# Expert-choice block on one core: another order of places for the streamed expert weights, and other moments and queues for three small loads

## Chip, cores, metric

One Trainium2 chip, one core of it. The time is that of one execution on the device, in microseconds; before and after are medians over runs. The profile is of one execution.

## What is computed

A diffusion block on 512 latent and 256 context tokens of width 1024 (float32, one layer). Two head groups (RWKV-7, 8 heads of 64, in both directions; gated linear attention) mix the tokens, an output projection and a norm follow, and then an expert-choice mixture of 16 SwiGLU experts (inner width 2816), each on its best 64 tokens:

```python
x = ln_affine(DN_ALPHA * x + g1 * (o_lat @ w_out), ln1_g, ln1_b)
h2 = modulate(ln_plain(x), sh2, sc2)
aff = softmax(h2 @ router_w)                       # (512, 16)
gates, idx = top_k(aff.T, 64)                      # each expert picks 64 tokens
y_e = (silu(h2[idx] @ w_gate[e]) * (h2[idx] @ w_up[e])) @ w_down[e]     # for 16 experts
x = ln_affine(DN_ALPHA * x + g2 * scatter_add(gates * y_e), ln2_g, ln2_b)
```

The expert weights are 16 x 3 x 1024 x 2816 float32 numbers, 553.6 MB; each is read once.

## The kernel before

One function, `body`, writes the whole program; a scheduler orders the instructions of each engine by their dependences and by priorities (`H(name)` raises one), and each engine then runs its list in order. Memory comes from pools in which a later tile takes the place of an earlier one and waits for the earlier one's last reader.

The stages that matter here:

- **Recurrence, to about 746 us.** RWKV runs over four strips of two heads (`b` = 0 to 3). Per strip: elementwise work (`rw_elem`, which loads two small weight tiles, `e_wr` and `e_ws`, in pool `zp0`), keys, an inverse of 24 triangular blocks (`rw_inverse`, L863 to L949) and twelve steps (`rw_step`, L969 to L1047), each of which needs the state of the step before. With strip 3 the scheduler fills TensorE's pauses with parts of the output projection.
- **Output projection, L1163 to L1210.** Its weights for heads 0 to 3 of the mix are eight tiles `w00` to `w31` (512 KB each, first number the 128 rows, second the column half), loaded by GpSimd at L1171. `product` (L1094) multiplies them, in three products each, since both sides are split into a high and a low part. Rows of x (`kx`, L1163) and gate rows (`zgs`, L1054) are loaded by SyncE.
- **Norm and router, L1215 to L1370.** For the four token tiles, in the order 1, 2, then 0, 3: statistics (L1247, L1255), norm with the factors `l1g` and `l1b` (each 128 x 1024, read broadcast from 4 KB; GpSimd's L1271 and VectorE's L1272 for tiles 1 and 2, VectorE's L1267 and L1274 for 0 and 3), second norm (L1263, L1265), transpose (L1343), router logits with `rwt` (L1348), softmax, and ranks by counting (L1303). `rwt` is made from the raw router weights `rwr` (128 x 8 x 16) by L1233 and L1242. L1366 is filler on TensorE that reads `hT` and `lgs`.
- **Experts, L1381 on.** `route(e)` gathers an expert's 64 tokens with one-hot products; `product_` multiplies them by eight gate tiles and eight up tiles of 128 x 2816 (L1439 loads, L1446 multiplies), then eight tiles of the down matrix follow (L1489, L1494). All are loaded by SyncE, in order, one tile after another, into twelve places of 12 KB per partition, `w0` to `w11`, which are taken round by round in the order of `wslot`. The places lie over what the earlier stages used: `w4`, `w5`, `w6` over arrays that the inverse of strip 3 reads last; `w7`, `w8`, `w9` over the recurrence's own of strips 1 and 3; `w0` to `w3` over the output projection's operands; `w10` over `hT` and `lgs`; `w11` over what the ranking reads.

A load waits until its place is free, and so does every load behind it on the same queue. SyncE's queue holds, in this order before the experts: the zgs loads (the last of them waits for strip 2's gate), `l1g` and `l1b` (which wait for the last recurrence step, as their pool lies over its arrays), the router's weights, and then the expert tiles.

```python
def vec(pl, name, src):                                    # L1217
    t = pl.tile([P, D], F32, name=name)
    EN[O("vq","s")].dma_start(t, src.to_broadcast([P, D]))
wslot = itertools.cycle((7, 8, 6, 4, 5, 2, 3, 1, 0, 11, 10, 9))        # L1384
wt = wp.tile([P, F], F32, name="wt", tag=f"w{next(wslot)}")            # L1438
ld = nc.sync.dma_start(wt, v[:, k])                                    # L1439
```

Of the kernel before, what the change touches and what calls it, by code (L numbers as in the profile page):

```python
# [8 lines left out]
F32 = mybir.dt.float32  # L9
# [3 lines left out]
OP = mybir.AluOpType  # L13
PSUM = bass.MemoryType.PSUM

OPT = dict(h_load=-100,h_rho=(0, 500, 60, 400),rh=(1, 2, 2, 2),b1=(0, 4),h_step=(0, 0, 0, 200),adb=4,h_post=(100, -100, 0),gf=512,h_rows=(0, 100),h_acc0=-100,h_scores=(500, 700, 0, -50),h_keys=(400, 500, 0, -100),b3=(0, 8),sp=1,gse='v',ea=1,f7=3,h_glah=0,bz=(10, 10),f3=1,r0b=0,fb=3,ge=0,p2=2,p1=0,f5=1,h_elem=(0, 700, 0, 60),f2=3,b2=(4, 0),h_inv=(200, 0, 0, 100),wo=(5, 6, 3, 4, 1, 2, 0, 8, 7),f8=3,f1=2,f6=1,h_split=0,f4=1,h_sub=(60, 60, 0, 150),h_out=(300, -100, 0, -200),h_crit=(700, 1000, 100, 400),vu='aa',h_lev=(150, 0, 0, 0),pwr=0,h_kv=(0, 0, 0, 0),h_post3=150)


def O(n, d):
    return OPT.get(n, d)  # L20


P = 128
D = 1024
KD = 8
# [3 lines left out]
E = 16  # L29
# [7 lines left out]
def body(tc, I, out):  # L37
    nc = tc.nc
# [18 lines left out]
    EN = dict(s=nc.sync, a=nc.scalar, g=nc.gpsimd)  # L57
# [3 lines left out]
    def pool(name, side, **kw):  # L61
        c = tc.tile_pool(name=name, bufs=1, side=side, reuse_waits="tile", **kw)
        return c, c.__enter__()
# [13 lines left out]
    def pss():  # L77
        return bank("s", 3)

    def pc():  # L80
        return bank("c", 3)
# [253 lines left out]
    for i in range(2):  # L335
        a = zpp.tile([P, 10, 66], F32, name=f"zpl{i}")
# [4 lines left out]
        a = zpp.tile([P, TC + 2], F32, name=f"zpc{i}")  # L341
# [158 lines left out]
    for d in range(2):  # L500
        for i in range(2):
            la, t = t3s[0:2]
            bias = ab[:, 2 * d + i:2 * d + i + 1]
            for lo, n in ((0, TC), (TC, TL)):
                p = pss()[:, 0:n]
# [13 lines left out]
            e = ebl[:, :, d, i]  # L519
# [13 lines left out]
    c_z0, zp0 = pool("rwz0", "left")  # L533
# [10 lines left out]
    wo = I["w_out"][0].rearrange("(k p) f -> p k f", p=P)  # L544
# [18 lines left out]
    for step in range(11):  # L563
# [12 lines left out]
        p = pc()  # L576
# [156 lines left out]
    def rw_elem(b, pss, fill=lambda n: None):  # L733
        with H("elem", b):
            return rw_elem_(b, pss, fill)
# [46 lines left out]
    e = rw_elem(0, pss, fill)  # L782
# [344 lines left out]
    with after(sub[0]) if O("ea", 1) else contextlib.nullcontext():  # L1127
        e = rw_elem(1, pe)
# [4 lines left out]
    for b in range(4):  # L1133
# [6 lines left out]
        if b < 2:  # L1140
            e = rw_elem(b + 2, pe)
# [73 lines left out]
    c_o, op_ = pool("outp", "right")  # L1215
# [5 lines left out]
        return t  # L1221

    hTs = [op_.tile([P, KD, P], F32, name=f"hT{i}") for i in range(2)]
    rwt = op_.tile([P, KD, 32], F32, name="rwt")
    rwr = op_.tile([P, KD, E], F32, name="rwr")
    sel = op_.tile([P, E], F32, name="sel")
    lgs = op_.tile([P, P], F32, name="lgs")
    sts = op_.tile([P, 8, 16], F32, name="sts")
    l1g, l1b = vec(op_, "l1g", I["ln1_g"]), vec(op_, "l1b", I["ln1_b"])

    EN[O("vq","s")].dma_start(rwr, I["router_w"][0].rearrange("(k p) e -> p k e", p=P))
    G.memset(rwt, 0.0)
    V.tensor_copy(rwt[:, :, 0:E], rwr)  # L1233

# [1 line left out]
    p = pe()  # L1236
# [89 lines left out]
    for part in ((1, 2), (0, 3)):  # L1326
        v = [x.rearrange("p (a b) -> p a b", b=P)[:, part[0]:part[1] + 1:part[1] - part[0]]
             for x in (mx[3][0], mx[3][1], ym[:, 3])]
        act(v[0], v[2], AF.Copy)
        V.tensor_tensor(v[1], v[2], v[0].bitcast(F32), op=S_)  # L1330
        for t in part:
# [4 lines left out]
            sp = t in (1, 2)  # L1336
# [3 lines left out]
            for k0 in (0, 4):  # L1340
                p = pe()
# [3 lines left out]
            p = pe()  # L1345
# [33 lines left out]
    def b2(tag, bufs, n=1):  # L1379
        return ps2.tile([P, 512 * n], F32, name="ps_" + tag, tag=tag, bufs=bufs)  # L1380

    c_m, mp = pool("moe", "left")
    c_w, wp = pool("wp", "left")
    wslot = itertools.cycle((7, 8, 6, 4, 5, 2, 3, 1, 0, 11, 10, 9))  # L1384
    for i in range(12):
        wp.tile([P, 3072], F32, name=f"w{i}")
    g2b = mp.tile([P, 512], F32, name="g2b")
# [39 lines left out]
    for e in range(E):  # L1427
# [35 lines left out]
        p = b2("m", 2)  # L1463
# [12 lines left out]
        for j0, n in GR:  # L1476
            p = b2("m", 2)
# [23 lines left out]
        if e == E - 1:  # L1501
            for t in range(4):
                for c in range(2):
                    p = b2(*(("m", 2) if t == 3 else ("gu", 6)))
# [53 lines left out]
```

## Time and profile before

| | |
|---|---|
| median of 3 runs | 2110.29 us (2107.8 to 2117.51) |
| profiled execution | 2105.25 us, its span 2103.5 us |
| TensorE busy | 1831.6 us, 87% of the span |
| VectorE, ScalarE, GpSimd busy | 769.4, 481.1, 315.7 us |
| mean DMA rate over the span | 302 GB/s |
| DMA rate in the span's slices 17 to 39 (of 40) | 424 to 426 GB/s |
| products with gate and up weights (L1446) | 689.2 us busy, 47.7 idle before them |
| products with down weights (L1494) | 311.4 us busy, 31.6 idle before them |

Busy times add up the instructions of one engine; matmuls are pipelined, so a busy TensorE is not one at its peak. A slice is 52.6 us. The expert stage fills the slices from 15 on; the ones before are bound by chains of small steps.

### The profile page before, as it was taken

The page shows a single profiled execution, that of the slowest core. Times are in us where ns is not written, and L with a number is a line of the kernel's source. Part 1 is how long each engine was busy: PE and PEld are TensorE (multiplying, and loading weights), DVE is VectorE, ACT ScalarE, POOL GpSimd, SP SyncE. Part 2 cuts the span into 40 slices and gives each one's busy share as a digit, 9 for nine tenths or more (in the row PEclk, how much of TensorE's full clock was granted, in tenths as well). Part 3 has the DMA queues.
Part 4 walks back from the last instruction along what each step waited for, and adds up shares of the span by engine and source line. Part 5 has one row for each costly group of instructions (what it writes and reads, how often), then busy time and mean ns, then how long its engine had stood idle before and what let it go on. Part 6 is the DMA issues. An engine that isn't in the chain of part 4 may idle for free. (4 is left out here: it accounts for less than half of the span.)

```text
span 2103.5 us, 31329 instructions
## 1 busy us (share of the span) xinstructions
PE 1831.6 (87%) x13266; PEld 936.1 (44%) x13266; DVE 769.4 (37%) x1445; ACT 481.1 (23%) x978; POOL 315.7 (15%) x318
## 2 busy tenths in 40 slices
PE   5898997788889988999998888988988888889886
PEld 1666776666667653333333333333333332333322
DVE  4676667766663262122112112122122121121113
ACT  2242445555652441011101101010010010011001
POOL 2543656343140220000000000000000000000001
PEclk8989998888897999999999999999999999999998
DMA  7645631510000268999999999999999999999995
GB/s 276 180 147 184 216 102 45 174 46 18 2 28 7 87 269 371 424 424 425 425 425 424 425 425 425 424 425 425 425 425 424 424 425 424 425 424 424 426 424 226
DMA packets 111416, 638.50 MB, mean 304 GB/s; under 512 B 13007, under 2 KB 40248, under 8 KB 60332
## 3 DMA queue, kind: packets, MB, share of 16 engines
q1 hardware_dynamic: 108944, 625.74, 73.1%
q0 software_dynamic: 2016, 10.49, 1.5%
q8 instruction: 104, 1.70, 0.3%
q10 hardware_dynamic: 316, 0.28, 0.0%
q14 instruction: 36, 0.29, 0.0%
HBM read 619.54 MB, written 15.75 MB: 302 GB/s over the span
## 5 line engine op out<-in xcount | busy, mean ns | idle before, releaser
L1446 PE MATMUL ps_gu<-wt,xT 128*64 128x512 f32 (+1 forms) x3072 | 689.2, 568 | 47.7 <-DMA wt<-in_ex_up_dram 35.7
L1446 PEld LDWEIGHTS ps_gu<-wt,xT 128*64 128x64 f32 x3072 | 239.2, 138 | 435.3 <-issue 292.4
L1494 PE MATMUL ps_gu<-wd,hT 128*64 128x512 f32 x1408 | 311.4, 595 | 31.6 <-DMA wd<-in_ex_down_dram 31.6
L1494 PEld LDWEIGHTS ps_gu<-wd,hT 128*64 128x64 f32 x1408 | 97.3, 137 | 233.8 <-issue 173.2
L1467 ACT ACTIVATE gT<-ps_m 128x512 f32<-128x512 f32 x16 | 9.6, 597 | 602.1 <-PE ps_m L45 602.1
L1508 DVE TENSOR_TENSOR ye<-ps_gu,g2b 128x512 f32<-128x512 f32 x16 | 11.1, 692 | 372.1 <-PE ps_gu L1494 372.1
L1297 POOL MEMSET cnt<- 128x12 f32 x16 | 1.6, 107 | 884.8 <-DVE rank L1319 872.7
L1409 PE MATMUL ps_m<-h,oh 128*64 128x512 f32 x256 | 93.1, 615 | 45.9 <-DVE oh L1404 45.9
L1520 DVE TENSOR_TENSOR kx<-kx,ps_m 128x512 f32<-128x512 f32 x120 | 77.1, 684 | 152.0 <-PE ps_m L1514 152.0
L298 PE MATMUL ps_d<-hh,wh 128*128 128x512 f32 (+1 forms) x336 | 127.3, 379 | 4.2 <-ACT kx L362 3.0
L298 PE MATMUL ps_d<-hh,wl 128*128 128x512 f32 (+1 forms) x336 | 122.5, 365 | 5.3 <-POOL wl L290 5.3
L298 PE MATMUL ps_d<-hl,wh 128*128 128x512 f32 (+1 forms) x336 | 123.6, 368 | 3.4 <-POOL hl L269 3.4
L88 DVE TENSOR_SCALAR hm<-hm 128x512 f32<-128x512 f32 (+1 forms) x48 | 19.5, 405 | 180.6 <-ACT hm L1458 180.6
L1411 ACT ACTIVATE xg<-ps_m 128x512 f32<-128x512 f32 x16 | 9.6, 597 | 330.1 <-PE ps_m L1409 330.1
L290 POOL TENSOR_TENSOR wl<-raw,wh 128x1024 fp32r<-128x1024 f32 x26 | 67.4, 2592 | 93.7 <-ACT wh L289 92.8
L1418 DVE TENSOR_TENSOR xT<-ps_m,mod 128x512 f32<-128x512 f32 x16 | 11.1, 692 | 188.5 <-PE ps_m L1414 188.5
L298 PEld LDWEIGHTS ps_d<-hh,wh 128*128 128x128 f32 x336 | 66.9, 199 | 25.8 <-issue 10.1
L298 PEld LDWEIGHTS ps_d<-hh,wl 128*128 128x128 f32 x336 | 67.2, 200 | 15.1 <-POOL wl L290 5.5
L298 PEld LDWEIGHTS ps_d<-hl,wh 128*128 128x128 f32 x336 | 66.9, 199 | 14.3 <-POOL hl L269 5.1
L1514 PE MATMUL ps_m<-ye,gT 64*128 64x512 f32 x244 | 68.8, 640 | 0.0
L1409 PEld LDWEIGHTS ps_m<-h,oh 128*64 128x64 f32 x256 | 28.9, 142 | 85.4 <-issue 77.6
L1303 DVE SCALAR_TENSOR_TENSOR scr<-ps_m,aff,lo 128x128 bf16<-128x128 f32 (+3 forms) x60 | 33.1, 551 | 91.6 <-PE ps_m L1399 90.0
(454 smaller groups left out, 2669.8 us busy)
## 6 DMA issues: line engine op xcount, KB each, us to landing
wt<-in_ex_gate_dram SPq DMA_DIRECT2D x128, 1408.0 KB, 26.4
wt<-in_ex_up_dram SPq DMA_DIRECT2D x128, 1408.0 KB, 27.1
wd<-in_ex_down_dram SPq DMA_DIRECT2D x96, 1536.0 KB, 27.6
wd<-in_ex_down_dram SPq DMA_DIRECT2D x32, 1024.0 KB
adat<-in_ada_w_dram SPq DMA_DIRECT2D x64, 256.0 KB, 3.0
raw<-in_w_in_dram SPq DMA_DIRECT2D x25, 512.0 KB, 3.8
adat<-in_ada_w_dram SPq DMA_DIRECT2D x4, 2048.0 KB
wo_d<-wx SPq DMA_DIRECT2D x16, 512.0 KB, 3.8
```

What stands on the lines that cost most here:

```text
L88: V.tensor_scalar(o, o, 1.0, 2.0 ** 60, op0=A, op1=OP.min)
L290: G.tensor_tensor(wl, raw, wh.bitcast(F32), op=S_)
L298: mm(p, a[:, k, :], b[:, k, lo:lo + n], start=k + i == 0, stop=k == KD - 1 and i == 2)
L1303: V.scalar_tensor_tensor(scr[:, l:h], row[:, l:h], aff[:, t, e:e + 1], (lo if before else hi)[:, z + l:z + h], op0=OP.is_ge if before else ...
L1409: mm(p[HR[h]], oh[:, t], h2[t][:, 512 * h:512 * h + 512], start=t == 0, stop=t == 3, skip_group_check=True)
L1411: act(xg, p, AF.Copy)
L1418: V.tensor_tensor(xv, p.rearrange("p (j h s) -> p j h s", j=4, h=2), sc, op=M)
L1446: i = mm(p[HR[h]], xT[:, k], wt[:, h * FH + f0:h * FH + f0 + w], start=k == 0, stop=k == KD - 1, skip_group_check=True)
L1494: mm(py[HR[c]], hT[:, j0 + j, 64 * h:64 * h + 64], wts[h][:, j, 512 * c:512 * c + 512], start=j0 + j + h == 0, stop=j0 + j == 10 and h == ...
L1508: V.tensor_tensor(ye, py, g2b, op=M)
L1514: mm(ps_[c], gT[HR[c], t * P:(t + 1) * P], ye[HR[c]], start=not last, stop=True, skip_group_check=True)
L1520: V.tensor_tensor(x, x, ps_[c], op=A)
```

## The change

Four edits:

- The option `vq` is `'a'`: `l1g` and `l1b` are issued on ScalarE's queue instead of SyncE's.
- The raw router weights and `rwt` no longer lie in the norm's pool `outp` but in `zp0`, in the places of `e_ws` and `e_wr`, which have had their last reader when strip 3's elementwise work has split them.
- The load of the raw router weights is written for SyncE's queue outright.
- The order of the twelve places begins with 6, 5, 4.

```diff
-OPT = dict(h_load=-100,
+OPT = dict(vq='a',h_load=-100,
...
-    rwt = op_.tile([P, KD, 32], F32, name="rwt")
-    rwr = op_.tile([P, KD, E], F32, name="rwr")
+    rwt = zp0.tile([P, 2 * KD, 32], F32, name="rwt", tag="e_ws")[:, 0:KD]
+    rwr = zp0.tile([P, 4 * KD, E], F32, name="rwr", tag="e_wr")[:, 0:KD]
...
-    EN[O("vq","s")].dma_start(rwr, I["router_w"][0].rearrange("(k p) e -> p k e", p=P))
+    nc.sync.dma_start(rwr, I["router_w"][0].rearrange("(k p) e -> p k e", p=P))
...
-    wslot = itertools.cycle((7, 8, 6, 4, 5, 2, 3, 1, 0, 11, 10, 9))
+    wslot = itertools.cycle((6, 5, 4, 7, 8, 9, 3, 2, 1, 0, 10, 11))
```

SyncE's queue, from the first zgs load to the first expert tiles (`kx` are rows of x, `wt` expert tiles):

```order
 L1163 DMA kx_7363<-xp_d 128x1024
 L1054 DMA zgs<-gg_d 128x512
+L1231 DMA rwr<-in_router_w_dram 128x8x16
 L1163 DMA kx_7365<-xp_d 128x1024
 L1163 DMA kx_7364<-xp_d 128x1024
```
```order
 L1163 DMA kx_7366<-xp_d 128x1024
 L1054 DMA zgs<-gg_d 128x512 x2
-L1220 DMA l1g<-in_ln_g_dram 128x1024
-L1220 DMA l1b<-in_ln_b_dram 128x1024
-L1231 DMA rwr<-in_router_w_dram 128x8x16
 L1439 DMA wt<-in_ex_gate_dram 128x2816 x8
```

The router's load moves forward behind the first zgs load; the expert tiles follow the last zgs load directly.

ScalarE, where the last recurrence step ends (L995) and the norm of the first token tiles begins:

```order
 L995 ACTIVATE VU<-ps_u 64x128 x2
 L1329 ACTIVATE mx_7351<-ym 128x256
+L1220 DMA l1g<-in_ln_g_dram 128x1024
+L1220 DMA l1b<-in_ln_b_dram 128x1024
 L1062 ACTIVATE zgs<-ym 128x2x128
```

The two loads of the norm's factors stand behind the first split of strip 3's mix and ahead of the second half of its group norm.

VectorE, at the statistics of the first token tiles (`kx_7364`, `kx_7365` are tiles 1 and 2):

```order
 L1255 BN_AGGR sts<-sts 128x2
-L1070 TENSOR_TENSOR ym<-ym,zgs 128x2x128
 L1259 SCALAR_TENSOR_TENSOR sts<-sts 128x1
-L1233 COPY rwt<-rwr 128x8x16
-L1247 BN_STATS sts<-ps_w 128x6
 L1241 COPY rbias<-ps_e 128x1
 L1242 TENSOR_TENSOR rwt<-rwt,mod_71 128x256
```

L1070, the last gating of strip 3 for token tiles 0 and 3, leaves its place ahead of L1259 and comes behind the first L1272; the copy of the router's weights goes to the third inverse, ahead of its transpose L891.

## Rows read from the trace of the kernel before

**Rows 1.** Stretch 1000 to 2060 us: busy by engine, clock, DMA share, GB/s

```profile
1000.00:2060.00 1060.00, 931.28 (x4514) 347.87 (x4512) 215.54 (x476) 95.94 (x198) 8.53 (x22) 1.00 1.01 425
```

**Rows 2.** Groups by line, TensorE, 840 to 2060 us: busy, mean ns | idle before

```profile
L1446 PE MATMUL ps_gu<-wt,xT 128*64 128x512 f32 (+1 forms) x2912 | 654.4, 567 | 47.2 <-DMA wt<-in_ex_up_dram 35.7 <-DMA wt<-in_ex_gate_dram 11.5
```

**Rows 3.** SyncE in order of time, 680 to 806 us: start, us, instruction

```profile
686.53 0.32 SPq L1054 DMA_DIRECT2D zgs<-gg_d  x1
...
746.65 0.33 SPq L1220 DMA_DIRECT2D l1g<-in_ln_g_dram  x1
...
747.98 27.04 SPq L1439 DMA_DIRECT2D wt<-in_ex_gate_dram  x8
...
803.16 2.69 SPq L1439 DMA_DIRECT2D wt<-in_ex_up_dram  x2
```

**Rows 4.** TensorE in order of time, the first expert products

```profile
800.53 26.20 PE L1446 MATMUL ps_gu<-wt,xT 128*64 128x512 f32 x132 [0.49 <-DVE xT L1419]
```

**Rows 5.** GpSimd in order of time, 685 to 704 us

```profile
685.72 0.59 POOL L1171 DMA_DIRECT2D w<-wo_d  x1
...
690.05 2.16 POOL L1171 DMA_DIRECT2D w<-wo_d  x4
```

**Rows 6.** DMA, GB/s in 40 slices of 685:691 and of 684:704; L1171's landing, 689:697

```profile
GB/s 0 0 0 0 109 0 0 0 0 0 0 0 0 164 137 82 27 191 191 273 355 300 328 410 437 355 355 396 314 355 314 178 41 27 14 0 0 0 0 0
...
GB/s 0 0 0 33 0 0 115 205 360 381 340 164 8 0 90 106 229 393 426 434 418 410 410 402 451 410 82 0 0 0 115 180 319 385 402 418 279 16 0 82
...
DMA to landing us min/median/max: 4.2/5.3/6.4
```

**Rows 7.** Stretches from 746 to 804.2 us, columns as in rows 1

```profile
746.00:794.00 48.00, 38.45 (x248) 26.37 (x249) 33.62 (x89) 21.21 (x51) 11.56 (x23) 0.89 0.74 295
...
794.00:798.00 4.00, 3.65 (x16) 1.26 (x16) 0.00 (x0) 0.28 (x1) 0.23 (x1) 1.00 0.92 329
...
798.00:802.00 4.00, 3.15 (x28) 1.88 (x30) 1.39 (x2) 0.91 (x2) 0.39 (x1) 1.00 0.92 358
...
802.00:804.20 2.20, 2.20 (x14) 0.73 (x12) 0.00 (x0) 0.00 (x0) 0.00 (x0) 1.00 1.01 417
```

**Rows 8.** TensorE in order of time, two steps of strip 3's recurrence

```profile
696.79 1.65 PE L1094 MATMUL ps_i<-w,mx 128*128 128x512 f32 x3
...
698.37 0.70 PE L984 MATMUL ps_w<-S,AM 128*64 128x64 f32 x8
...
701.21 0.96 PE L1094 MATMUL ps_i<-w,mx 128*128 128x512 f32 x3
```

**Rows 9.** Stretch 762 to 766 us, columns as in rows 1

```profile
762.00:766.00 4.00, 2.11 (x9) 1.68 (x9) 3.98 (x6) 2.61 (x4) 2.77 (x6) 0.76 1.01 431
```

**Rows 10.** L701 by line; VectorE in order of time, 573 us; L1233 by tile

```profile
L701 DVE TENSOR_TENSOR e_ws<-e_wr,e_ws x1: 681/681/681, 508.2 to 508.2; 32x512 fp32r<-32x512 f32 x1
...
573.13 1.25 DVE L891 STREAM_TRANSPOSE t<-X 128x1024 f32<-128x1024 f32 x1
...
L1233 DVE COPY rwt<-rwr x1: 221/221/221, 753.3 to 753.3; 128x128 f32<-128x128 f32 x1
```

**Rows 11.** 743 to 779 us in order of time: TensorE, ScalarE, VectorE, GpSimd

```profile
743.26 0.29 PE L1040 MATMUL ps_k<-RM,S 128*64 128x64 f32 x4
...
748.48 0.42 ACT L1062 ACTIVATE zgs<-ym 128x256 f32<-128x256 f32 x1 [1.31 <-DVE ym L1061]
...
752.91 0.42 DVE L1070 TENSOR_TENSOR ym<-ym,zgs 128x256 f32<-128x256 f32 x1 [1.13 <-POOL ym L1069]
...
775.16 0.54 DVE L1265 TENSOR_SCALAR h<-kx,sts 128x512 f32<-128x512 f32 x1
...
777.83 1.41 DVE L1267 SCALAR_TENSOR_TENSOR kx<-ps_k,sts,l1g 128x512 f32<-128x512 f32 x2
...
755.20 2.55 POOL L1271 TENSOR_TENSOR kx<-kx,l1g 128x1024 f32<-128x1024 f32 x1 [2.32 <-ACT kx L1263]
```

More of the change, by code (lines that the diff above doesn't have):

```diff
@@ L14 @@
 PSUM = bass.MemoryType.PSUM
-OPT = dict(h_load=-100,h_rho=(0, 500, 60, 400),rh=(1, 2, 2, 2),b1=(0, 4),h_step=(0, 0, 0, 200),adb=4,h_post=(100, -100, 0),gf=512,h_rows=(0, 100),h_acc0=-100,h_scores=(500, 700, 0, -50),h_keys=(400, 500, 0, -100),b3=(0, 8),sp=1,gse='v',ea=1,f7=3,h_glah=0,bz=(10, 10),f3=1,r0b=0,fb=3,ge=0,p2=2,p1=0,f5=1,h_elem=(0, 700, 0, 60),f2=3,b2=(4, 0),h_inv=(200, 0, 0, 100),wo=(5, 6, 3, 4, 1, 2, 0, 8, 7),f8=3,f1=2,f6=1,h_split=0,f4=1,h_sub=(60, 60, 0, 150),h_out=(300, -100, 0, -200),h_crit=(700, 1000, 100, 400),vu='aa',h_lev=(150, 0, 0, 0),pwr=0,h_kv=(0, 0, 0, 0),h_post3=150)
+OPT = dict(vq='a',h_load=-100,h_rho=(0, 500, 60, 400),rh=(1, 2, 2, 2),b1=(0, 4),h_step=(0, 0, 0, 200),adb=4,h_post=(100, -100, 0),gf=512,h_rows=(0, 100),h_acc0=-100,h_scores=(500, 700, 0, -50),h_keys=(400, 500, 0, -100),b3=(0, 8),sp=1,gse='v',ea=1,f7=3,h_glah=0,bz=(10, 10),f3=1,r0b=0,fb=3,ge=0,p2=2,p1=0,f5=1,h_elem=(0, 700, 0, 60),f2=3,b2=(4, 0),h_inv=(200, 0, 0, 100),wo=(5, 6, 3, 4, 1, 2, 0, 8, 7),f8=3,f1=2,f6=1,h_split=0,f4=1,h_sub=(60, 60, 0, 150),h_out=(300, -100, 0, -200),h_crit=(700, 1000, 100, 400),vu='aa',h_lev=(150, 0, 0, 0),pwr=0,h_kv=(0, 0, 0, 0),h_post3=150)
 def O(n, d):
```

## The prediction, made before the change was run

> **What bounds the kernel now.** Read the expert stage first, in the view of busy time by stretches [rows 1]: from 1000 to 2060 us the DMA engines are taken for 1.01 of the time and move 425 GB/s, while TensorE has gaps. The groups by line say whose gaps: the gate and up products stand idle for 47.2 us, all of it before a weight's landing [rows 2]. So the expert stage lasts as long as 553.6 MB of expert weights take, and the whole kernel ends a fixed tail after the last of them. What counts is when the unbroken stream begins, and how many bytes have moved before.
>
> A weight tile (one of the 16 gate or up tiles of an expert) is 1408 KB or 1.442 MB, 3.4 us at 425 GB/s. It goes into one of twelve places, and a place that is taken is free again only when the tile in it has been multiplied. SyncE's row in order of time [rows 3] has the first gate tile at 747.98 us, because l1g, issued at 746.65, stands ahead of it in the queue, and the next issue of SyncE before that is at 686.53. The thirteenth goes out at 803.16. That moment is TensorE's: its first expert product starts at 800.53 [rows 4] and it has done with tile 1, 12 of the 132 matmuls in 26.20 us, 2.4 us later. From 803.16 on nothing stops the stream.
>
> **Early tiles: what they are worth.** In the new order the first three places (6, 5, 4) hold arrays that the last inverse was the last to use, and the router's and the norm's loads stand no longer ahead. So tiles 1 to 3 follow the load at 686.53 at once, 60 us earlier. Tiles 4 to 6 wait for products of the last recurrence step, tiles 7 to 12 for the same late work as now (output projection, TensorE's filler on hT, ranking). All twelve will be in their places before 803, and then SyncE must wait for TensorE as it does now. The gain is therefore not 60 us, nor three tiles, but what today is still missing from twelve tiles when the thirteenth begins to move, about 804.2 (issue plus some 1 us: GpSimd's load of 685.72 [rows 5] moves from 687.0 on [rows 6]).
>
> Today, by the stretches [rows 7]: 746 to 794 us 48 x 295 = 14.16 MB, less l1g and l1b (1.05) and the router (0.07), is 13.04 MB or 9.05 tiles. From 794 to 804.2: 4 x 329 + 4 x 358 + 2.2 x 417 = 3.67 MB, less 0.26 for g2b, is 2.36 tiles. Together 11.4. With twelve done the stream is 0.6 tile ahead: **-2.0 us**. This holds as long as TensorE begins at 800.53.
>
> **What the three tiles collide with.** They go out at about 686.9, 687.3 and 687.7. GpSimd issues the output projection's weights in the same stretch [rows 5]: one 512 KB load at 685.72 and four (w01, w10, w11, w30) from 690.05. Today these have the engines for themselves and land after 4.2 to 6.4 us [rows 6]. TensorE has their products, as filler, in order among those of the last recurrence: the third product of the row at 696.79 (about 697.8) is the first that reads w10, and L984 of the recurrence's step follows at 698.37 directly behind it [rows 8]. A late w10 holds up the recurrence, and each step waits for the one before, so the delay reaches 800.53 whole. The first load and the zgs load of 686.53 have moved by 690.1 [rows 6]. If transfers of the two queues then take turns: tile 1, w01, tile 2, w10 take 3.4 + 1.24 + 3.4 + 1.24 us, to 699.4, and 0.8 for the landing (the four of today have moved by 697.2, the last lands 698.0): 700.2, 2.4 us late. Then tile 3 and w11: 704.8 against 701.5 + 2.4, another 0.9. The later ones are in time. **+3.3 us.** Bounds: 0, if GpSimd's loads went first; 5.8, if the three tiles went first (w01 at 702.3 against 696.8, w10 0.3 more).
>
> Do two queues share at all? The slices of 0.15 us from 685 to 691 hold loads of both queues, and none is over 437 GB/s, one queue's rate later [rows 6]; that is one limit for both, though it doesn't say who goes first. The Trainium skill, DMA: Bandwidth & Descriptors, Issuing engines are not separate DMA queues, says that transfers started by ScalarE, SyncE and GpSimd run on the same 16 engines and interleave. By that rule the stall stays in the sum, +2.3 in all; with queues of their own it would be -1.0. The trace agrees as far as the shared limit.
>
> A wait also costs clock: where TensorE was busy for 2.11 of 4 us, the granted clock was 0.76 [rows 9]; 0.24 x 4 = 1 us at most for a pause of this size. I take 0 and keep 1.0 for the upper end.
>
> **The router's weights.** SyncE issues them behind the first zgs load, when the places they take are read out: the last reader is at 508.2, and the copy on VectorE now stands before the transpose at 573.13 [rows 10], so nobody waits for the landing. The copy, 0.22 us today [rows 10], and a clearing on GpSimd move from the tail to there. **0**, at most +0.2 on the third inverse's chain.
>
> **The tail from 746 to 800.** l1g and l1b go out on ScalarE behind L1329, two issues of 0.33 us (SyncE's today) to some 0.4, into its pause of 1.31 us before L1062 at 748.48 [rows 11]. What waits is GpSimd's product with l1g at 755.20. Tiles 4 to 6 can leave from about 743.6 (the place of tile 4 is read last by L1040 of the last step, 743.26). Taking turns, tiles 4 and 5 move from 744.6 to 751.4, then l1g to 752.6: in time. If all three went first, 754.8 + 1.24 + 0.8 = 756.8, 1.6 late. On VectorE the order changes: L1259 no longer stands behind L1070, which idled 1.13 us at 752.91; and the two L1265 of the first token tile come ahead of L1267 of the last, at 777.83 today, 0.54 us each. The last token tile's chain ends the stage, so I take **+1.0**; bounds -1.1 and 1.0 + 1.6 = 2.6.
>
> **Sum.** -2.0 + 3.3 + 1.0 = +2.3 us. The profiled execution took 2105.25 us (span 2103.5), 5.0 under the median 2110.29 of the three runs; it would become 2107.6, and the median **2112.6**. Low end: -2.0 + 0 - 1.1 = -3.1, 2107.2; high end: -2.0 + 5.8 + 2.6 + 1.0 = +7.4, 2117.7. The runs before lie 2.5 below and 7.2 above their median, so I put 2 us more on the low side: 2105 to 2118. A measurement tells about 0.5% from no change, 10.6 us.
>
> **Rivals.**
> 1. *The places don't limit.* If SyncE could send the thirteenth tile as soon as the twelfth has moved, about 797 to 798, three whole tiles would be won: -10.2 + 3.3 + 1.0 = -5.9, 2104.4; without the stall -10.2, 2100.1, at the border of what can be told. For it: the stream is the bound everywhere else. Against: the issue at 803.16, just when tile 1 is multiplied. Chance 0.07.
> 2. *No collision.* GpSimd's loads get through, because a queue with a few small transfers is served beside a long one: -2.0 + 1.0 = -1.0, 2109.3. For it: the loads keep 4.2 us beside zgs. Against: 4.3 MB of tiles and 2.1 MB of loads want the same 15 us. Chance 0.2.
> 3. *Slower: first come, first served.* The three tiles go first. Place: TensorE's row at 696.79, where w01 is then missing for 5.5 us and w10 for 0.3 more; the same again with l1g behind tiles 4 to 6 (1.6), and the clock. -2.0 + 5.8 + 2.6 + 1.0 = +7.4, 2117.7. It decides against the change as soon as stall and tail together exceed 2.0 us, and could be told from no change only above 12.6. Chance 0.2.
> 4. *The change doesn't do what it says.* A wait that I have not seen keeps tile 1 until 743; then no stall, but also nothing moved early, and still twelve tiles by 798: -1.0, 2109.3. Chance 0.05.
>
> **How the numbers follow.** The forecast has 0.48; all cases but the outer half of rival 1 and an extreme of rival 3 lie within 0.5%. Faster by over 0.5%: 0.03 (rival 1 without the stall). Slower: 0.05 (rival 3, if pauses lengthen each other). The rest, 0.92, is no change that can be told. 2105 to 2118 leaves out rival 1 and some 0.1 of scatter.
>
> **What would show it.** Three tiles at 687 to 688 on SyncE and the next only at 743 to 747; GpSimd's four loads landing 2 to 6 us later; TensorE held before the product that reads w10, and the recurrence's end near 750; six more tiles around 775, a hole in the DMA slices between the twelfth tile and the first expert product, which starts at 803 to 806 instead of 800.53; from there the same 425 GB/s. Wrong would be: a thirteenth tile issued before the first L1446; a first L1446 at or before 800.5; or an expert stage that is shorter by itself.

## The result, and the profile after

| | before | after |
|---|---|---|
| median, us | 2109.05 of 14 runs (2099.78 to 2119.86) | 2119.32 of 14 runs (2106.63 to 2127.2) |
| profiled execution, its span | 2105.25, 2103.5 | 2122.24, 2120.5 |

The ratio is 1.0056, 95% interval [1.0034, 1.0077]: some 12 us slower (the two medians lie 10.3 us apart), where 2.3 us were forecast. The median is 1.3 us above the forecast's high end.

The stream of weights is what it was [rows 1]. The stretch view of the changed kernel, the same 1060 us counted from the later start, and the 13 us ahead of the thirteenth tile:

```profile
1015.00:2075.00 1060.00, 945.04 (x4529) 353.67 (x4526) 217.68 (x479) 95.94 (x198) 8.52 (x22) 0.98 1.01 425
...
808.00:821.20 13.20, 10.63 (x73) 5.73 (x73) 4.57 (x16) 1.20 (x3) 0.62 (x1) 1.00 0.57 221
```

425 GB/s at a share of 1.01 again; and ahead of 821 us the engines are taken for 0.57 of the time: the hole that the forecast has, with twelve tiles in their places and the thirteenth waiting for TensorE. SyncE and TensorE in order of time [rows 3, 4]:

```profile
691.66 0.32 SPq L1054 DMA_DIRECT2D zgs<-gg_d  x1
692.15 99.50 SPq L1439 DMA_DIRECT2D wt<-in_ex_gate_dram  x8
...
808.24 20.42 SPq L1439 DMA_DIRECT2D wt<-in_ex_up_dram  x6
```
```profile
818.62 26.20 PE L1446 MATMUL ps_gu<-wt,xT 128*64 128x512 f32 x132 [0.49 <-DVE xT L1419]
```

Three tiles leave right behind the last zgs load (692.15, 692.57 and 693.00), the fourth at 756.75, as said. Tiles 7 to 12 leave between 790.8 and 811.4, later than the forecast's 775 or so, and still ahead of the first product. The first expert product starts at 818.62 instead of 800.53: **+18.1 us** in this pair of executions, and all of the loss is ahead of it. Not all of it belongs to the change: strip 2's first step already starts at 616.9 instead of 610.0, when of the four edits only the router's have acted, and the eight kernels below, which all have the router's edits, have it anywhere between 608.6 and 614.7 (last section). So each kernel is measured from a point behind that stretch, GpSimd's first load of the output projection (L1171): A from there to the end of the recurrence (first split of strip 3, L1329), B from there to the first expert product, C from there to the last byte of expert weights (the end of its packet). A and B are differences of starts in the trace, of one execution each, in us; the clock is the mean that TensorE was granted over B:

| kernel | A | B | clock in B | C | sum against before | ratio measured |
|---|---|---|---|---|---|---|
| before | 61.0 | 53.8 | 0.90 | 1275.9 | 0 | |
| the change | 69.0 | 58.8 | 0.88 | 1274.7 | +11.8 | 1.0056 [1.0034, 1.0077] |
| router_only | 61.4 | 54.8 | 0.88 | 1275.7 | +1.2 | 0.9997 [0.9973, 1.0021] |
| hold3 | 61.4 | 58.3 | 0.88 | 1274.4 | +3.4 | 0.9998 [0.9975, 1.0021] |
| hold6 | 69.1 | 55.3 | 0.88 | 1274.4 | +8.2 | 1.0041 [1.0017, 1.0064] |
| hold_both | 61.0 | 56.5 | 0.85 | 1274.1 | +1.0 | 1.0022 [0.9997, 1.0047] |
| quarter | 63.7 | 54.6 | 0.91 | 1274.6 | +2.2 | 1.0013 [0.9986, 1.0039] |
| one_early | 63.7 | 59.5 | 0.86 | 1274.3 | +6.9 | 1.0025 [0.9996, 1.0054] |
| old_places | 61.0 | 60.0 | 0.86 | 1275.8 | +6.1 | 1.0048 [1.0021, 1.0075] |
| gpsimd_hold | 60.8 | 54.0 | 0.91 | 1274.0 | -1.9 | 1.0004 [0.9978, 1.0030] |

The change's sum, +11.8 us, is 0.56% of 2109, which is what the runs say. It has three parts: +8.0 in A, +5.0 in B, -1.2 in C. In every kernel the sum lies within the interval of its measured ratio.

**A, the recurrence.** TensorE's waits by line from 688 to 712 us (us in total, times, longest), then the same engine in order of time:

```profile
PE ps_i L1094 <- DMA w<-wo_d: 3.9, 2, 3.4
PE ps_i L946 <- issue: 3.1, 1, 3.1
```
```profile
701.44 0.20 PE L946 MATMUL ps_i<-SC,yh 32*32 32x32 f32 x1 [3.12 <-issue]
...
705.35 1.19 PE L1094 MATMUL ps_i<-w,mx 128*128 128x512 f32 x2 [0.54 <-DMA w<-wo_d]
...
709.94 0.80 PE L1094 MATMUL ps_i<-w,mx 128*128 128x512 f32 x1 [3.40 <-DMA w<-wo_d]
710.67 0.70 PE L984 MATMUL ps_w<-S,AM 128*64 128x64 f32 x8
```

The lower two pauses are the ones that the forecast described: the product that reads w10 waits, and L984, the recurrence's step, stands directly behind it [rows 8]. The first pause it did not have. In the middle of the inverse's last products (L946) TensorE stands for 3.12 us and waits for no semaphore ("issue"). The DMA view has a queue of kind "instruction" that moves 16 KB at a time. Its row before the change, from 690.7 to 692.0 us, and after it, from 699.0 to 700.2 us (packets, MB, share):

```profile
q8 instruction: 1, 0.02, 4.2%
```
```profile
q8 instruction: 1, 0.02, 4.9%
```

Before, this packet begins 0.29 us after the first L946 and L946 does not stop; after, 3.23 us after it, and TensorE goes on 1.4 us after the packet's end. From 695.2 to 698.9 us the changed kernel's DMA view has one row, the tiles' queue:

```profile
q1 hardware_dynamic: 175, 1.41, 98.3%
```

So a block of code came late while SyncE's queue, with the first tile, had the engines to itself. That it is TensorE's is read from its moment: over all ten kernels the pause goes with this packet, from none where it begins 0.9 us ahead of the first L946 (gpsimd_hold) to 3.1 us where it begins 3.2 us behind it. The code is not alone in this. GpSimd's w01, issued at 695.17, moves its first packet 3.7 us later; before, 1.3 us after its issue.

The pauses are not three prices to be added. The product that reads w10 starts 12.1 us after GpSimd's first load before (697.8 [rows 8] less 685.72) and 19.1 us after (709.94 less 690.85), as soon as w10 has landed, 14.2 us after its issue. These 7.0 us are the price of the late w10, and the pause in L946 lies inside them: with its code in time, TensorE would have stood for w01 and w10 until 709.9 all the same, as GpSimd had issued both before the pause began. (No run has the late weights without the late code; this is read from the landing.) Nearly all of the other 1.0 us of A's 8.0 follows directly, in the 34 matmuls from that step's L984 to its L1003, before and after (the clock is the third value from the end):

```profile
698.37:700.83 2.46, 2.46 (x34) 1.56 (x33) 0.29 (x1) 0.54 (x2) 0.59 (x2) 0.83 0.71 175
```
```profile
710.67:713.95 3.28, 3.28 (x34) 2.04 (x33) 0.29 (x1) 0.54 (x2) 0.00 (x0) 0.54 1.01 373
```

They take 0.8 us longer at a granted clock of 0.54 instead of 0.83.

**B, the tail.** ScalarE, GpSimd, VectorE and ScalarE again in order of time [rows 11]:

```profile
759.96 0.36 ACTq L1220 DMA_DIRECT2D l1g<-in_ln_g_dram  x1
...
770.26 2.34 POOL L1271 TENSOR_TENSOR kx<-kx,l1g 128x1024 f32<-128x1024 f32 x1 [3.21 <-DMA l1g<-in_ln_g_dram]
...
773.14 1.23 DVE L1272 TENSOR_TENSOR kx<-kx,l1b 128x1024 f32<-128x1024 f32 x1 [4.84 <-DMA l1b<-in_ln_b_dram]
774.29 2.56 DVE L1070 TENSOR_TENSOR ym<-ym,zgs 128x256 f32<-128x256 f32 x1
...
776.88 0.42 ACT L1329 ACTIVATE mx<-ym 128x256 fp32r<-128x256 f32 x1 [7.10 <-DVE ym L1070]
```

GpSimd can start 10.3 us after l1g's issue and has waited 3.2 us for it, VectorE 4.8 for l1b. As with w01, l1g's first packet moves only 3.6 us after the issue; in hold6 below, with no tile under way, it moves after 1.0. Behind the waiting L1272 stands L1070, the gating of token tiles 0 and 3; ScalarE's split waits 7.1 us for it. The two splits of strip 3 are 17.0 us apart (759.87 and 776.88), 6.6 us before.

What this costs is read from kernels with a like clock in B. Late loads: 58.8 (the change) and 58.3 (hold3) against 55.3 (hold6, loads in time, the order of the change), 3.0 to 3.5 us, about GpSimd's wait. The order on VectorE and ScalarE: 55.3 against router_only's 54.8, and quarter's 54.6 against 53.8 (before) and 54.0 (gpsimd_hold), 0.5 to 0.8 us, although the order alone puts the two splits 13.8 us apart (hold6). The remaining 1.0 us goes with the clock, 0.88 instead of 0.90: router_only, without the new order and without a late load, has it too.

### The profile page after: what moved, and what is told of

It is laid out like the page before. It is cut to its first block, busy times and chain, and to the rows that moved or that the text cites. A ratio compares the mean times of both kernels' runs of the same rounds, so it can differ in the third digit from the quotient of the medians.

```text
span 2120.5 us, 31334 instructions
## 1 busy us (share of the span) xinstructions
PE 1846.1 (87%) x13266; PEld 941.8 (44%) x13266; DVE 774.9 (37%) x1445; ACT 480.7 (23%) x978; POOL 313.0 (15%) x318
## 5 line engine op out<-in xcount | busy, mean ns | idle before, releaser
L1446 PE MATMUL ps_gu<-wt,xT 128*64 128x512 f32 (+1 forms) x3072 | 704.5, 577 | 49.6 <-DMA wt<-in_ex_up_dram 35.5
L1409 PE MATMUL ps_m<-h,oh 128*64 128x512 f32 x256 | 99.1, 640 | 45.9 <-DVE oh L1404 45.9
```

The source lines that it names most:

```text
L1409: mm(p[HR[h]], oh[:, t], h2[t][:, 512 * h:512 * h + 512], start=t == 0, stop=t == 3, skip_group_check=True)
L1446: i = mm(p[HR[h]], xT[:, k], wt[:, h * FH + f0:h * FH + f0 + w], start=k == 0, stop=k == KD - 1, skip_group_check=True)
```

## Experiments

Each kernel is compared with runs of the kernel before on the same chip. A "hold" is a transfer of 128 bytes on SyncE that reads a tile: SyncE waits until that tile is written, and what stands behind it waits too. In hold3, hold6 and hold_both the order of the instructions on each engine is otherwise that of the change. Each diff is shown in part; the holds' 128 bytes go to a small array `fen_d`, whose line is left out.

**hold3**, tiles 1 to 3 behind the last weight of the output projection:

```diff
-    split(2)
+    split(2); fen1 = nc.sync.dma_start(fen_d[0:1, 0], oaw[2][1][0:1, 0, 0:32].bitcast(F32))
...
-                ld = nc.sync.dma_start(wt, v[:, k])
+                with after({0: fen1}[k]) if e == 0 and name == "ex_gate" and k in (0,) else contextlib.nullcontext(): ld = nc.sync.dma_start(wt, v[:, k])
```

> The change, with SyncE kept from issuing the first three expert tiles until the last weight load of the output projection (w21) has landed: a 128-byte transfer that reads w21 stands ahead of them. Theory 1 (two collisions, first with GpSimd's loads, then with l1g and l1b): the first collision is gone, so the recurrence ends 5 us earlier than in the change against the start of strip 3's steps, w10 lands within 7 us of its issue, and the time is 3 us over before, ratio 1.0015. Theory 2 (7 us of the loss lie ahead of 690 us, in the moved router work): strip 2 still starts 7 us late and the ratio stays at 1.003. Theory 3 (the collision does not hold TensorE, the clock does): w10 early and yet the same 13 us at the recurrence's end, ratio 1.0056.

Measured: A 61.4, as before; ratio 0.9998. TensorE's wait for w is gone, and the pause in L946 is 0.4 us. Theory 1 holds; strip 2 started at 612.2 and the ratio is not 1.003, so theory 2 falls, and so does theory 3: without the collision the 8 us are gone.

**hold6**, tiles 4 on behind the first token tile's norm, tiles 1 to 3 early as in the change:

```diff
-                ld = nc.sync.dma_start(wt, v[:, k])
+                with after(ld) if k else contextlib.nullcontext(): fen2 = nc.sync.dma_start(fen_d[0:1, 1], x1[1][0:1, 0:32]) if e == 0 and name == "ex_gate" and k == 3 else None
+                with after(fen2) if fen2 is not None else contextlib.nullcontext(): ld = nc.sync.dma_start(wt, v[:, k])
```

> The change, with SyncE kept from issuing the fourth expert tile until the first token tile's norm is done (a 128-byte transfer that reads it stands ahead of tile 4). Theory 1: l1g and l1b have the engines for themselves and land 4 to 6 us after their issue instead of 10 to 13, GpSimd's first product with l1g no longer waits for a load, the time from the recurrence's end to the first expert product falls from 58.7 us to about 54 to 55, ratio 1.003 with the first collision still there. Theory 2: the order on VectorE and ScalarE is what costs in the tail, not the late loads: still 57 us or more, ratio 1.005.

Measured: A 69.1 with the same two pauses (3.9 and 3.1 us), B 55.3 instead of 58.8, ratio 1.0041. GpSimd's L1271 waits for no load any more. The late loads are some 3.4 us of the tail; 1.5 stay over before. Theory 2, which had 57 us or more, falls.

**hold_both**, both holds:

> Both holds: tiles 1 to 3 behind w21's landing, tiles 4 on behind the first norm; the order on every engine is otherwise that of the change. Theory 1: no collision is left, and the 0.6 tile ahead counts: -2 to +1 us against before, ratio 0.999 to 1.0005. Theory 2: 7 us ahead of 690 us remain, ratio 1.003.

Measured: A 61.0, B 56.5, C 1274.1, sum +1.0; ratio 1.0022 [0.9997, 1.0047], whose interval holds what either theory said. A and C are theory 1's: nothing is left of the first stall, and the early tiles' worth is there. B stays 2.7 us over before though l1g is in time. The order, with L1070 still behind L1272, is that of hold6, which has 55.3; the 1.2 us between the two go with the clock, 0.85 against 0.88.

**router_only**, the router's part of the change alone:

```diff
-OPT = dict(vq='a',
+OPT = dict(
...
-    wslot = itertools.cycle((6, 5, 4, 7, 8, 9, 3, 2, 1, 0, 10, 11))
+    wslot = itertools.cycle((7, 8, 6, 4, 5, 2, 3, 1, 0, 11, 10, 9))
```

> Only the router's part of the change: its weights early in the other memory, but l1g and l1b on SyncE's queue and the old order of places, so no expert tile is early. Theory 1: nothing waits for it, the start of strip 2 is where it was within the scatter of runs, ratio 1.000 (0.999 to 1.001). Theory 2: strip 2 starts 7 us late here too, ratio 1.0033.

Measured: 0.9997, A 61.4, C 1275.7. Strip 2's first step starts at 613.9. The router's move costs nothing that can be told. Theory 2 is out by the ratio, whose interval ends at 1.0021.

**quarter**, the first three tiles in four transfers each:

```diff
-                ld = nc.sync.dma_start(wt, v[:, k])
+                for q in range(4 if e == 0 and name == "ex_gate" and k < 3 else 1): ld = nc.sync.dma_start(wt[:, 704 * q:704 * q + 704], v[:, k, 704 * q:704 * q + 704]) if e == 0 and name == "ex_gate" and k < 3 else nc.sync.dma_start(wt, v[:, k])
```

> The change, with each of the first three expert tiles loaded as four transfers of 704 columns: packets of 2816 bytes in place of 11264, everything else alike. Theory 1 (two queues take turns packet by packet, so a queue's share follows its packets' size): GpSimd's 4096-byte packets get 59% of the engines instead of 27%, w10 lands 8 to 10 us after its issue instead of 14.2, TensorE waits for it under 1 us instead of 3.9, and the fetch of TensorE's code, which was 3.1 us late, waits behind smaller packets, under 1 us: from the first weight load of the output projection to the recurrence's end 63 to 65 us instead of 70.3, ratio about 1.002 to 1.003. Theory 2 (shares go by transfers or by order of arrival, not by packets): 70 us again, ratio 1.0055.

Measured: A 63.7, ratio 1.0013. TensorE does not wait for w at all, but the pause in L946 is 2.8 us. The edit did more than cut the packets: only six of the twelve transfers left early, one and a half tiles. SyncE's waits between 699 and 775 us have the seventh, which leaves at 767.58, waiting for l1g:

```profile
SPq L1439 <- DMA l1g<-in_ln_g_dram: 61.2, 1, 61.2
```

So A here is not the price of three tiles in small packets; the shares can be read from the packets alone. On them theory 1 is right, on the code it is wrong. The queues while both are busy, hold6 from 703 to 711 us (tiles whole) and quarter from 708 to 712 us:

```profile
q1 hardware_dynamic: 243, 2.40, 73.1%
q0 software_dynamic: 240, 0.92, 30.7%
```
```profile
q0 software_dynamic: 246, 0.94, 63.0%
q1 hardware_dynamic: 260, 0.65, 46.4%
```

The two queues move the same number of packets, 243 and 240, 260 and 246; GpSimd's queue, with 4096 bytes in each, gets 0.92 of 3.32 MB (28%) beside packets of 11264 bytes and 0.94 of 1.59 (59%) beside packets of 2816. Turns are taken by packet, once both queues move. The Trainium skill, DMA: Bandwidth & Descriptors, Queues, rings and completion order, has each engine go round its queues packet by packet; these counts agree, the first 3.7 us of w01 without a packet do not show it. In B quarter has 54.6: l1g, issued at 763.47, met no tile, as the next one left only behind it.

**one_early**, one tile early:

```diff
-    wslot = itertools.cycle((6, 5, 4, 7, 8, 9, 3, 2, 1, 0, 10, 11))
+    wslot = itertools.cycle((6, 7, 8, 9, 5, 4, 3, 2, 1, 0, 10, 11))
```

> The change with the order of places 6, 7, 8, 9, 5, 4, then as it was: only one expert tile is early, the next waits for the last recurrence step. Theory 1 (the stall lasts as long as tiles are moving): one tile has moved before w01 is asked for, so TensorE waits for w10 under 0.5 us, for its code 0 to 2 us: 62.5 to 64.5 us from the first weight load to the recurrence's end (62.2 before, 70.3 in the change); the tail is no better than in the change, since five tiles stand ahead of l1g: 57 to 59 us; the early tile's worth stays, since all twelve are in by then. Ratio 1.002. Theory 2 (any early tile costs the 8 us): 70 us, ratio 1.0056.

Measured: A 63.7: no wait for w, but 2.9 us in L946. B 59.5. C 1274.3, as low as with three tiles. Theory 1 holds for w, not for the code: one tile makes it late as much as three do. Here, as in quarter, w10 lands while TensorE stands for its code (13.3 and 14.1 us after GpSimd's first load, where the product was due at 12.1), so the pause also covers a wait of 1 to 2 us for w10.

**old_places**, the change with the old order of places (the `wslot` line of router_only's diff alone):

> The change with the old order of places: no expert tile is early, l1g and l1b on ScalarE's queue. Theory 1: no first stall (62.3 us from the first weight load to the recurrence's end), but two to five tiles leave when the last step's products are done and l1g, l1b get 27% of the engines beside them: tail 56 to 59 us against 52.3 before, no gain: +4 to +6 us, ratio 1.002 to 1.003. Theory 2 (the tail's price is the new order on VectorE and ScalarE alone): 54 to 55 us, ratio 1.001.

Measured: A 61.0, B 60.0, C 1275.8, ratio 1.0048. With no tile early the first stall is gone and the tail is at its worst: five tiles stand ahead of l1g. Theory 2 falls.

**gpsimd_hold**, hold_both with l1g and l1b on GpSimd's queue (`vq='g'`):

> A version without collisions: tiles 1 to 3 behind w21's landing, tiles 4 on behind the first norm, l1g and l1b on GpSimd's queue, which leaves VectorE's order at L1070 as it was before the change. Theory 1: first stall 0 (62.3 us), tail 52 to 53.5 us, early tiles -1.5 us: -1.5 to 0 us, ratio 0.9993 to 1.000. Theory 2: GpSimd stands waiting for the place of l1g and the gating behind it comes late: tail 55 us or more, ratio 1.001.

Measured: A 60.8, B 54.0, C 1274.0: -1.9 us by the trace, ratio 1.0004 [0.9978, 1.0030]. It is the one version with all of the early tiles' worth and none of their price; by the runs it cannot be told from the kernel before. VectorE in order of time, and GpSimd:

```profile
762.47 0.43 DVE L1070 TENSOR_TENSOR ym<-ym,zgs 128x256 f32<-128x256 f32 x1 [0.66 <-POOL ym L1069]
767.20 1.23 DVE L1272 TENSOR_TENSOR kx<-kx,l1b 128x1024 f32<-128x1024 f32 x1
```
```profile
764.76 2.40 POOL L1271 TENSOR_TENSOR kx<-kx,l1g 128x1024 f32<-128x1024 f32 x1 [2.33 <-ACT kx L1263]
```

L1070 stands ahead of L1272 again, nothing waits for a load, and the tail is that of before. Not all of the 2.5 us against hold_both is the order's: the clock in B is 0.91 here and 0.85 there. Quarter, which has hold_both's order and a clock of 0.91, is 0.6 us longer than this. No run has the order alone.

## Why the prediction was wrong

- **What bounds the kernel, and what early tiles are worth: right.** The twelve places limit; the worth was put at -2.0 us and is -1.2 in the change, -1.5 to -1.9 where tiles are held. The thirteenth tile left only after the first product. Rival 1 is out.
- **The step that failed first: "If transfers of the two queues then take turns", and with it "+3.3 us. Bounds: 0, if GpSimd's loads went first; 5.8, if the three tiles went first".** A grew by 8.0, and the product that reads w10 came 7.0 us late. The first turn is as forecast: w01 moves when the first tile is nearly through. From there the turns are by packet and not by transfer: w01 takes some 4.8 us where 1.24 were forecast, its packets of 4096 bytes between the tiles' of 11264, and w10 gets 28% of the bytes in its turn and comes with the third tile. It lands 14.2 us after its issue, where turns by transfer gave 9.6 and the bound with the three tiles first about 13. That TensorE's waits for w add up to 3.9, near the forecast's 3.3, is luck: it came to them 3.0 us late, after the pause in L946 (0.39 us before, 3.41 after, from one start to the next). That pause, TensorE's own code, had no term; in the change it lies inside w10's 7.0 us, and in one_early, where w10 was nearly in time, it is what A shows (2.7 us). The last 1.0 us goes with the clock, which was taken as 0 with 1.0 kept for the upper end.
- **The second: "Taking turns, tiles 4 and 5 move from 744.6 to 751.4, then l1g to 752.6: in time", and with it "+1.0; bounds -1.1 and 1.0 + 1.6 = 2.6".** B grew by 5.0. From 764 to 768 us the queues of SyncE and ScalarE moved 105 packets each, 11264 against 4096 bytes:

```profile
q1 hardware_dynamic: 105, 1.00, 65.9%
q10 hardware_dynamic: 105, 0.43, 31.1%
```

  so l1g ends during the third tile, not behind the second, and GpSimd's product waits 3.2 us for it, twice the bound's 1.6. hold6 takes 3.4 us of B away. The order, forecast at +1.0 with the loads in time, is worth 0.5 to 0.8. L1070 and ScalarE's split, which the forecast does not name, do come late by it, and the stage hardly feels it. The remaining 1.0 us goes with the clock; the forecast has no term for the clock in the tail outside its high end.
- **The router, 0: right** as far as can be told (0.9997 [0.9973, 1.0021]).
- **The rivals.** Rival 3's direction came true, and by its place, and its rule in part: the first tile goes first, and then the queues share. Rival 2 would need a queue of small transfers to be served first; here the queue with the smaller packets gets the smaller share. Rival 4 is out: the three tiles left when they were to. The sum -2.0 + 3.3 + 1.0 reads, measured, -1.2 + 8.0 + 5.0.

Open: why a transfer that starts on another queue while tiles stream gets nothing for 3.5 to 3.8 us, whether the tiles' packets are large or small. Where tiles are early, w01's first packet and the code's begin within 0.3 us of each other, 3.3 to 3.9 us behind the tiles' first packet, in the change, hold6 and one_early (11264 bytes) as in quarter (2816).

## What to carry to other kernels

A transfer moved into an idle stretch is not free there because the engines are idle on average: list what else asks for bytes in that stretch, the small loads that an in-order engine stands in front of, and the engine's own code. What a small load gets beside a long one goes, once both move, by the size of the packets, so a long transfer that must share can be cut into narrow pieces; but its start was late here with small pieces too. What removed the price was to hold the long transfer behind the last small one by a short transfer that reads it, as hold3 does. Two pauses in a row on one engine are priced by when the last thing waited for lands, not by adding them. And where an order changes, look at the end of the stage: a split that comes 7 us later by the order alone costs 0.5 to 0.8 here.

## What the runs showed of the hardware that was not expected

- Code moves on a DMA queue of its own, 16 KB at a time, and has to share the engines with the data: with a single weight tile ahead of it TensorE stands for 2.8 to 3.1 us in a stretch of short matmuls, with nothing but "issue" in the profile. That the code is TensorE's is inferred from the moment, in ten kernels.
- A transfer that starts beside a stream of tiles moves its first packet 3.5 to 3.8 us after its issue (w01, l1g), instead of 1.0 to 1.3. From then on the queues share by equal counts of packets (243 and 240, 105 and 105).
- Most of the scatter between these traces has one place. The stretch from strip 2's first step to the first L1171's wait has the same 1028 matmuls in every kernel and takes 65.1 us at the least (hold3) and 83.8 at the most (hold6, quarter, gpsimd_hold). The stretch view of hold3, hold_both and hold6:

```profile
612.20:677.30 65.10, 60.41 (x1028) 45.20 (x1028) 33.67 (x90) 28.99 (x75) 8.82 (x15) 0.98 0.02 6
```
```profile
613.60:686.60 73.00, 68.31 (x1028) 50.58 (x1028) 33.67 (x90) 29.00 (x75) 8.82 (x15) 0.85 0.02 5
```
```profile
609.70:693.50 83.80, 79.21 (x1028) 59.23 (x1028) 33.92 (x90) 29.31 (x75) 8.82 (x15) 0.68 0.02 5
```

  The clock granted over the stretch is 0.98, 0.85 and 0.68. In hold6 it stands at 0.50 (1.2 GHz) from about 634 to 682 us with TensorE busy all the time, behind a pause (busy for 2.06 us between 629.7 and 633.7); in hold3 it stays at 1.00 (2.4 GHz) behind a like one (2.11 us between 632.2 and 636.2). What makes the difference is open. With 19 us between the ends, a comparison of two single executions of this kernel says little unless it starts behind this stretch; the sums above do.
